# Where one modulation vector's matrix-vector product is computed: layer 1's mixer gate, in the recurrence or in layer 0's second channel product

## The chip, the core and the metric

The kernel runs on one core of a Trainium2 chip. The core has five engines that run side by side, each through its own queue of instructions in order: TensorE (PE; the loading of its stationary operand is listed apart as PEld), VectorE (DVE), ScalarE (ACT), GpSimd (POOL) and SyncE (SP), which here only issues DMA transfers. Data comes from DRAM into an on-chip memory of 128 partitions; matmul results go to banks of a second, small memory (PSUM) and are fetched from there by VectorE or ScalarE.

The metric is device time in microseconds (us), lower is better. Three timed runs of the kernel before gave 2395.1, 2395.52 and 2399.87 us, median 2395.52.

## The reference

A trunk of two layers on x (1 sequence × 1024 positions × 1024 channels, float32). Each layer has a token mixer (layer 0: softmax attention with forgetting; layer 1: gated linear attention, a recurrence over chunks) and a channel mixer of 2816 hidden channels. Both are fed a normalised input that is shifted and scaled, and their results are gated, by six vectors that are computed from a conditioning vector c:

```python
c_act = silu(c)
for i in range(2):
    mod = c_act @ ada_w[i] + ada_b[i]          # ada_w[i]: 1024 x 6144
    sh1, sc1, g1, sh2, sc2, g2 = split(mod, 6)
    h = rms_norm(x, norm1_g[i]) * (1 + sc1) + sh1
    y = forgetting_attention(h, ...) if i == 0 else gated_linear_attention(h, ...)
    x = x + g1 * y
    h = rms_norm(x, norm2_g[i]) * (1 + sc2) + sh2
    gate, up = split(h @ ffn_w_in[i], 2)
    x = x + g2 * ((silu(gate) * up) @ ffn_w_out[i])
return rms_norm(x, final_g)
```

So there are 12 modulation vectors of 1024 numbers, each a product of c_act with a 1024 × 1024 block of `ada_w` (4 MB). They depend on c alone and may be computed at any time before their use. The one at issue is (layer 1, j = 2): g1 of layer 1, which multiplies the recurrence's output projection.

## The kernel before

**Precision.** A float32 matmul is made of three products of a reduced type: each operand is split into a high part (a cast on ScalarE, line 174) and a low part (a subtraction on VectorE, line 175), and `mm3` (lines 286 to 288) adds high·high, high·low and low·high. So nearly every weight and activation passes through ScalarE and VectorE before TensorE can use it.

**Stages.** Layer 0's attention ends before 690 us of the profiled execution. Its channel mixer's first product runs to about 1012 us, its second product to about 1180, and the rest of that mixer, with the norm for the next layer, to about 1290. The recurrence of layer 1 follows, with its last head up to about 1690. Layer 1's channel mixer takes what is left.

**The channel mixer, `ffn`.** Both products use a scheme of seven block products in place of eight, with sums and differences of blocks as operands (names such as T1, T2, B11). The first product runs through groups of hidden channels, `for X in gs[2:]`. A finished hidden block is written to DRAM (`hid_d`). The second product runs over three chunks of hidden channels, the third of them followed by four hidden tiles that are multiplied plainly; a chunk makes 28 products (`p_`), each of 9 matmuls (3 × `mm3`). While one chunk is multiplied, the operands of the next are read back from `hid_d` by `part(c_)`: most directly into their tile (line 1607), those that still need a split through a ring of raw views, `late_raw` (split in line 1382 or 175). `late_raw` has four views: three in `tmpv`, and `opr_["u"][0]`, one slot of the operands of the first product that is free by then. The same ring serves `load_xr` (line 1631), which reads the mixer's input back for the final addition. The weights come through `feed`, some products ahead, as a raw view `xv` that is split into `o`. The results `p_b` are added up on VectorE (line 1521 in the first product, 1698 in the second) or copied out by ScalarE.

**A modulation vector, `ada_steps(l, j, acc, raw_of, nt, ahead)`.** On the paths at issue nt is 2, and a vector takes 32/nt = 16 steps. A step takes a raw view of 128 × 512, issues four loads of 64 KB into it on SyncE's queue (line 423), and then makes two multiply-adds on VectorE, 128 × 256 each (line 442 for a vector's first, line 444 for the others), which add `raw × c` to the sum `acc`. `ahead` is the number of steps whose loads are issued before the first multiply-add: with `len(raws_)` raw views it is one less. After 16 steps two small matmuls with a 128 × 4 operand of ones (`mp`, line 449) sum over the partitions, and one addition on VectorE (line 452) puts the vector into `modc`.

**Pace.** The steps are a generator that the main work drives. `Pace` counts units of TensorE's work: each product of the channel mixer calls `ada1(0.64 * n)`, 1.92 units for a product of 9 matmuls, and the recurrence calls `ada1(5.1)` once per projection. A step costs `ADA_A` units before its multiply-adds and `ADA_B` after them; `flush` runs all that is left at once. The multiply-adds are tied behind the VectorE instruction that was written last (`issue_after(last_of("D"))`).

**Where each vector of layer 1 is computed before.** j = 0 and 1 in layer 0's first channel product (`mid(0, 1)`, three raw views, pace 6.0 + 3.0); j = 2, 3 and 4 in the recurrence (`ada1_queue((2, 3, 4), ...)`, two raw views, pace 2.6 + 1.0); j = 5 in layer 1's first channel product (pace 12 + 6).

**What sets the order.** The program is written as one stream. A scheduler then puts the instructions of each engine into an order, with a simulated timeline, keeping the dependences between tiles and the ties that the code states. SyncE's loads go out in that order too. A change in one place can thus move instructions elsewhere.

**The recurrence.** Per head: projections (`gv_body`, `head_front`, `r_proj`), the gate with its exponentials and logarithms on ScalarE (lines 1859 and 1860) and a scan on VectorE (line 1864), a state `Sf` that is updated on VectorE (line 1942) and split for TensorE (`S_t`), and an output `on_t` (line 1990) that is transposed by TensorE (line 1952).

## Time and profile before

| | |
|---|---|
| median of three runs | 2395.52 us (2395.1 to 2399.87) |
| the profiled execution, its own time | 2397.77 us |
| its span in the profile | 2396.1 us |
| granted TensorE clock, mean | 0.997 |
| busy: PE, VectorE, ScalarE, GpSimd | 2368.3, 1776.6, 1127.8, 1008.5 us |
| DMA | 363.42 MB, mean 152 GB/s |

The profile is one execution. It gives for each engine the time in which it was busy, and for a group of instructions (one source line, one operation, one pair of tiles) the count, busy sum and mean. Tile names say what is moved: `ad_s` is the raw view and the sum of a modulation vector, `p_b` a product in PSUM, `xv_s` a raw weight, `o_s` a split weight. A row of a window's table gives, for a stretch of the span, the busy time of each engine. Rows of the timeline give start, duration, engine, line and operation; a bracket at the end tells the idle time before an instruction and what ended it. A row of waits reads: engine and waiting instruction, what released it, and then the idle time in us, the number of such waits and the longest. A row of DMA issues gives count, size and the median time from issue to landing.

### The profile page before, as it was taken

The numbers are of one execution on the slowest core, as the hardware profiler recorded it, in microseconds if no ns is written. First come the engines' busy times: TensorE is split into PE (matmuls) and PEld (weight loads), VectorE is DVE, ScalarE is ACT, GpSimd is POOL, SyncE is SP. The second block draws the span as 40 slices with busy tenths as digits, with TensorE's granted clock in tenths as the row PEclk, the third lists the DMA queues.
The fourth block names the chain that finished last, engine by engine and source line by source line (L and its number), as shares of the span: only waits on it lengthen the run. The fifth ranks groups of instructions, "written<-read, shape, count | busy, mean of one in ns | idle before, by whom it ended". The sixth has DMA issues, their size and how long they took to land.

```text
span 2396.1 us, 35784 instructions
## 1 busy us (share of the span) xinstructions
PE 2368.3 (99%) x12344; PEld 2016.8 (84%) x12344; DVE 1776.6 (74%) x3016; ACT 1127.8 (47%) x2164; POOL 1008.5 (42%) x911
## 2 busy tenths in 40 slices
PE   8999999999999999999999999999999999999998
PEld 7888888888888888888888888898888888888888
DVE  6577878886698788876798666655687877775787
ACT  6666555674443333345325645353343333345326
POOL 1333333333445666643264321222345666643262
PEclk9999999999999999999999999999999999999999
DMA  7422424342435544557655242334424544457664
GB/s 254 145 89 90 131 84 128 106 138 83 150 109 173 179 166 165 171 196 261 229 187 162 67 119 80 107 112 135 136 96 161 183 145 159 154 182 256 228 202 146
DMA packets 335773, 363.42 MB, mean 152 GB/s; under 512 B 24348, under 2 KB 277432, under 8 KB 335592
## 3 DMA queue, kind: packets, MB, share of 16 engines
q1 hardware_dynamic: 335592, 361.15, 45.9%
q8 instruction: 97, 1.59, 0.3%
q14 instruction: 84, 0.69, 0.1%
HBM read 268.19 MB, written 92.86 MB: 151 GB/s over the span
## 4 chain that ended last, share of the span: by engine, by line
PE 90%; DVE 5%; DMA 2%; ACT 1%; issue 1%; POOL 0%; SPq 0%; DVEq 0%; POOLq 0%; ACTq 0%
PE p_b L288 16%; PE p_b L286 16%; PE p_b L287 16%; PE t_b L1164 2%; PE o_b L1178 2%; PE qk_b L286 2%; PE qk_b L287 2%; PE qk_b L288 2%; PE vps_b L286 1%; PE vps_b L288 1%; PE vps_b L287 1%; PE s_b L1132 1%; PE s_b L1133 1%; PE gr_b L286 1%; PE gr_b L287 1%
## 5 line engine op out<-in xcount | busy, mean ns | idle before, releaser
L175 DVE TENSOR_TENSOR o_s<-xv_s,o_s 128x512 fp32r<-128x512 f32 (+1 forms) x376 | 324.1, 867 | 66.1 <-ACT o_s L174 65.6
L174 ACT CAST o_s<-xv_s 128x512 fp32r<-128x512 f32 (+1 forms) x376 | 216.2, 587 | 303.6 <-PE p_b L288 248.0
L287 PE MATMUL p_b<-B,o_s 128*128 128x512 f32 x608 | 237.8, 391 | 0.0
L288 PE MATMUL p_b<-B,o_s 128*128 128x512 f32 x608 | 237.5, 391 | 0.0
L286 PE MATMUL p_b<-B,o_s 128*128 128x512 f32 x608 | 236.3, 392 | 0.0
L1144 POOL TENSOR_SCALAR lp_s<-lp_s,st 128x128 f32<-128x128 f32 (+7 forms) x128 | 99.0, 778 | 291.1 <-DVE st L1143 280.7
L843 POOL TENSOR_TENSOR ex_s<-xv_s,xv_s 128x512 f32<-128x512 f32 (+1 forms) x64 | 85.5, 1335 | 292.8 <-DMA xv_s<-in_ffn_w_in_dram 120.7
L286 PE MATMUL p_b<-T,o_s 128*128 128x512 f32 x480 | 186.7, 389 | 0.0
L287 PE MATMUL p_b<-T,o_s 128*128 128x512 f32 x480 | 186.7, 389 | 0.0
L288 PE MATMUL p_b<-T,o_s 128*128 128x512 f32 x480 | 181.2, 389 | 0.0
L287 PEld LDWEIGHTS p_b<-B,o_s 128*128 128x128 f32 x608 | 115.0, 189 | 23.9
L286 PEld LDWEIGHTS p_b<-B,o_s 128*128 128x128 f32 x608 | 115.0, 189 | 23.8
L288 PEld LDWEIGHTS p_b<-B,o_s 128*128 128x128 f32 x608 | 114.7, 189 | 24.0
L1142 ACT ACTIVATE lp_s<-lp_s,st 128x128 f32<-128x128 f32 (+7 forms) x128 | 99.3, 777 | 65.2 <-DVE st L1138 62.1
L174 ACT CAST pt_s<-t_b 128x512 fp32r<-128x512 f32 (+1 forms) x160 | 79.7, 547 | 75.4 <-PE t_b L1164 73.9
L845 POOL TENSOR_TENSOR xv_s<-ex_s,xv_s 128x512 f32<-128x512 f32 (+1 forms) x64 | 88.1, 1377 | 60.7 <-DVE o_s L175 58.2
L1521 DVE TENSOR_TENSOR ex_s<-ex_s,p_b 128x512 f32<-128x512 f32 x140 | 93.7, 681 | 23.4 <-PE p_b L288 23.2
L227 POOL TENSOR_TENSOR w_l_s<-w__s,w_h_s 128x256 fp32r<-128x256 f32 x90 | 69.7, 803 | 94.7 <-ACT w_h_s L223 56.7
L175 DVE TENSOR_TENSOR pt_s<-t_b,pt_s 128x512 fp32r<-128x512 f32 (+1 forms) x160 | 96.2, 631 | 15.9 <-ACT pt_s L174 15.3
L287 PEld LDWEIGHTS p_b<-T,o_s 128*128 128x128 f32 x480 | 90.1, 188 | 18.7
L286 PEld LDWEIGHTS p_b<-T,o_s 128*128 128x128 f32 x480 | 90.1, 188 | 18.7
L288 PEld LDWEIGHTS p_b<-T,o_s 128*128 128x128 f32 x480 | 90.1, 188 | 18.6
(1954 smaller groups left out, 7392.9 us busy)
## 6 DMA issues: line engine op xcount, KB each, us to landing
xv_s<-in_ffn_w_in_dram SPq DMA_DIRECT2D x176, 256.0 KB, 3.3
hid_B<-x SPq DMA_DIRECT2D x70, 512.0 KB, 2.6
ad_s<-in_ada_w_dram SPq DMA_DIRECT2D x384, 64.0 KB, 2.4
hid_T<-x SPq DMA_DIRECT2D x36, 512.0 KB, 2.8
xv_s<-in_ffn_w_out_dram SPq DMA_DIRECT2D x96, 192.0 KB, 5.3
ada_s<-in_ada_w_dram SPq DMA_DIRECT2D x128, 128.0 KB, 2.8
xv_s<-in_ffn_w_out_dram SPq DMA_DIRECT2D x40, 256.0 KB, 2.9
T2o<-hid_T SPq DMA_DIRECT2D x18, 512.0 KB, 8.4
```

The source lines that it names most:

```text
L174: nc.scalar.copy(hi, src)
L175: nc.vector.tensor_sub(lo, src, hi.bitcast(F32))
L227: (nc.gpsimd if i < 3 else nc.vector).tensor_sub(lo[:, cs], rw[:, cs], hi[:, cs].bitcast(F32))
L286: nc.tensor.matmul(ps, ah, bh, start=start, stop=False)
L287: nc.tensor.matmul(ps, ah, bl, start=False, stop=False)
L288: nc.tensor.matmul(ps, al, bh, start=False, stop=stop)
L843: nc.gpsimd.tensor_add(s1, a21, a22)
L845: nc.gpsimd.tensor_sub(a11, s1, a11)
L1142: nc.scalar.activation(lp, lp, AF.Exp, bias=mcur, scale=-1.0, accum_out=st[:, qi, 2:3])
L1144: nc.gpsimd.tensor_scalar(lp, lp, st[:, qi, 3:4], 1.0, op0=ALU.mult, op1=ALU.mult)
L1164: nc.tensor.transpose(tp[:, i, :], lps[qi][:, psl(2 * b + jj)], ident)
L1521: nc.vector.tensor_add(d, d if src is None else dest(G, src), ps)
```

## The change

Vector (layer 1, j = 2) leaves the queue of the recurrence and becomes a queue of layer 0's `ffn`, started at the last but one group of its first product and driven by the products of the second. There it has one raw view, the slot half `opr_["u"][0]`, and `opr_["u"][1]` holds the sum; so `ahead` is 0, and a step's loads can only go out when the multiply-adds of the step before have read the view. Its pace is 5.0 + 2.5 units. A flush before the last chunk makes sure that it is done. `late_raw` loses that view and has three; `load_xr`, which comes later, has the four as before. The recurrence keeps j = 3 and 4, with the pace 4.0 + 1.4 in place of 2.6 + 1.0. The tests on `ahead` in `ada_steps` become tests on `nt`, so that a vector with `ahead` = 0 still yields before its multiply-adds.

```diff
-            if ahead:
+            if nt == 2:
                 yield ADA_A
             raw = got.popleft()
             with ExitStack() as es:
-                if ahead:
+                if nt == 2:
                     es.enter_context(tc.issue_after(last_of("D")))
...
-            yield ADA_B if ahead else 1.0
+            yield ADA_B if nt == 2 else 1.0
...
-    def ada1_queue(js, acc, raws_):
+    def ada1_queue(ljs, acc, raws_):
         r = Cycle(raws_)
-        for j in js:
-            ada1.q.append(ada_steps(1, j, acc, r, 2, len(raws_) - 1))
+        for l, j in ljs:
+            ada1.q.append(ada_steps(l, j, acc, r, 2, len(raws_) - 1))
...
-    def ffn(l, oh, xs, slots, nm, mid, norm_end, each=None):
+    def ffn(l, oh, xs, slots, nm, mid, norm_end, each=None, later=()):
...
-        late_raw = Cycle(list(tmpv) + [opr_["u"][0]])
+        late_raw = Cycle(list(tmpv))
+        xr_raw = Cycle(list(tmpv) + [opr_["u"][0]])
...
-                    xr[(a, hf)] = late_raw()
+                    xr[(a, hf)] = xr_raw()
...
             if X is gs[-2]:
                 ada1.flush()
+                if later:
+                    ada1_queue(later, opr_["u"][1][:, 0:256], opr_["u"][0:1])
+                    ada_rate(5.0, 2.5)
                 nxt[0] = part(0)
                 advance(4)
...
         for c_ in range(OC):
             last = c_ == OC - 1
+            if last:
+                ada1.flush()
...
+    def ada_rate(a, b):
+        nonlocal ADA_A, ADA_B
+        ADA_A, ADA_B = a, b
...
-    ffn(0, oh, xs, slots, "fo", lambda: mid(0, 1), norm_mixer)
+    ffn(0, oh, xs, slots, "fo", lambda: mid((1, 0), (1, 1)), norm_mixer, later=((1, 2),))
...
-    ada1_queue((2, 3, 4), ada_v[0][:, 0:256], ada_v[1:3])
-    ADA_A, ADA_B = 2.6, 1.0
+    ada1_queue([(1, j) for j in (3, 4)], ada_v[0][:, 0:256], ada_v[1:3])
+    ADA_A, ADA_B = 4.0, 1.4
```

More of the change, by code (lines that the diff above doesn't have):

```diff
@@ L1760, in norm_mixer, with mid @@
         return gates
-    def mid(*js):
-        v = Views(slots["hid"], 2, [HALF], f"ad{js[0]}").v
-        ada1_queue(js, v[0][:, 0:256], v[1:4])
+    def ada_rate(a, b):
+        nonlocal ADA_A, ADA_B
+        ADA_A, ADA_B = a, b
+    def mid(*ljs):
+        v = Views(slots["hid"], 2, [HALF], f"ad{ljs[0][0]}").v
+        ada1_queue(ljs, v[0][:, 0:256], v[1:4])
     ADA_A, ADA_B = 6.0, 3.0
-    ffn(0, oh, xs, slots, "fo", lambda: mid(0, 1), norm_mixer)
+    ffn(0, oh, xs, slots, "fo", lambda: mid((1, 0), (1, 1)), norm_mixer, later=((1, 2),))
     h1 = hs1
@@ L2102, in trunk @@
     ADA_A, ADA_B = 12.0, 6.0
-    ffn(1, oh, xs, slots, "go", lambda: mid(5), final_norm, final_scale)
+    ffn(1, oh, xs, slots, "go", lambda: mid((1, 5)), final_norm, final_scale)
     dump("xb1", xs)
```

## The prediction, made before the changed kernel was run

> **What bounds the kernel now.** The page comes first: span, busy time, and the chain of work that ended last.
>
> ```profile
> span 2396.1 us, 35784 instructions
> ...
> PE 2368.3 (99%) x12344; PEld 2016.8 (84%) x12344; DVE 1776.6 (74%) x3016; ACT 1127.8 (47%) x2164; POOL 1008.5 (42%) x911
> ...
> PE 90%; DVE 5%; DMA 2%; ACT 1%; issue 1%; POOL 0%; SPq 0%; DVEq 0%; POOLq 0%; ACTq 0%
> ```
>
> TensorE bounds the program: 28 us of the span have no matmul in them. A change that adds and removes no large matmul can only win back such idle time, or make more of it. So the second view is the busy time by stage (us, then each engine with its count, granted clock, DMA share, GB/s). The stages are layer 0's first channel product, its second product, the end of that mixer, and the recurrence up to its last head.
>
> ```profile
> core 0: us, PE busy (x) PEld busy (x) DVE busy (x) ACT busy (x) POOL busy (x), PEclk, DMA share, GB/s
> 690.00:1012.00 322.00, 322.00 (x1426) 266.72 (x1425) 266.61 (x353) 121.73 (x214) 198.41 (x132) 1.00 0.52 173
> 1012.00:1180.00 168.00, 168.00 (x742) 139.08 (x742) 112.30 (x159) 69.74 (x132) 68.15 (x54) 1.00 0.61 218
> 1180.00:1290.00 110.00, 109.43 (x489) 90.24 (x489) 98.21 (x138) 38.44 (x71) 51.46 (x41) 1.00 0.61 199
> 1290.00:1600.00 310.00, 306.15 (x1888) 274.46 (x1887) 198.48 (x363) 159.37 (x340) 81.30 (x94) 0.99 0.35 101
> ```
>
> The stage that gives the work away, 1290 to 1600, has 310.00 − 306.15 = 3.85 us of PE idle time: the whole prize. The stage that takes it, 1012 to 1180, has none: there the change can only be free or cost. Its VectorE is idle for 168 − 112.3 = 55.7 us.
>
> **The change, part by part.** First, what the gate g1 of layer 1 costs where it is. The rows of the modulation tile within the recurrence:
>
> ```profile
> L423 SPq DMA_DIRECT2D ad_s<-in_ada_w_dram x192: 560/592/1827, 1302.2 to 1586.0; - x192
> L444 DVE SCALAR_TENSOR_TENSOR ad_s<-ad_s,c,ad_s x48: 467/485/1049, 1344.9 to 1589.3; 128x256 f32<-128x256 f32 x48
> L444 DVE SCALAR_TENSOR_TENSOR ad_s<-ad_s,c x45: 461/484/1054, 1343.1 to 1587.5; 128x256 f32<-128x256 f32 x45
> ...
>   DMA ad_s<-in_ada_w_dram: 25.9, 14
> ...
> DMA to landing us min/median/max: 2.2/2.4/6.5
> ```
>
> Three vectors make 192 loads and 96 multiply-adds there; one third leaves: 64 loads (64 × 0.592 = 37.9 us of SyncE's issuing) and 32 multiply-adds (32 × 0.485 = 15.5 us of VectorE). VectorE also sat idle 25.9 us, 14 times, for these loads; with the slower pace of the two that stay (4.0 + 1.4 for 2.6 + 1.0, one load ahead as before), a load has 9.4 units instead of 6.2 before its use, so most of these waits go too. What is that worth to PE? The PE waits of the stage, and what ended them:
>
> ```profile
> PE go_b L286 <- ACT S_t L174: 1.4, 1, 1.4
> PE ogt_b L1952 <- DVE on_t L1990: 1.1, 2, 0.8
> PE go_b L286 <- ACT junk L1986: 1.0, 1, 1.0
> PE gr_b L286 <- DVE gvt_s L175: 0.4, 1, 0.4
> ```
>
> None is ended by a modulation instruction. The queue of ScalarE ahead of the 1.4 us wait (PE at 1398.07):
>
> ```profile
> 1393.00 1.28 ACT L1859 ACT_TABLE_LOAD   x1
> 1394.29 1.06 ACT L1859 ACTIVATE t_s<-t_s 128x1024 f32<-128x1024 f32 x1
> 1395.37 1.28 ACT L1860 ACT_TABLE_LOAD   x1
> 1396.66 1.06 ACT L1860 ACTIVATE t_s<-t_s 128x1024 f32<-128x1024 f32 x1
> 1397.63 0.39 ACT L174 CAST S_t<-Sf 128x256 fp32r<-128x256 f32 x1
> ...
> 1403.10 0.41 ACT L174 CAST S_t<-Sf 128x256 fp32r<-128x256 f32 x1 [2.94 <-DVE Sf L1942]
> ```
>
> Two table loads and two gate functions (4.7 us) stand in front of the cast of the state. The 1.0 us wait has the same source: the cast at 1403.10 came late because VectorE ran the gate's scans:
>
> ```profile
> 1400.29 2.33 DVE L1864 TENSOR_TENSOR_SCAN b_s<-ad_s,t_s 128x512 f32<-128x512 f32 x2
> ```
>
> A multiply-add of 0.485 us stands between such steps only here and there. So lighter VectorE work in the recurrence gives at most 3.85 us back and, from these rows, little of it; the other end is a new wait as long as the longest shown, +1.4, because the program's order in this stage is made anew. I take −0.5, near the rows that name the gate as cause. The cover of the 32 multiply-adds that went was PE's own work; nothing else was late for them.
>
> Second, the cost where the gate goes. The pace is 5.0 + 2.5 units a step, 16 steps, from the last but one group of the first product until about 1180. There is one buffer (the other half of a slot holds the sum), so a step's four loads wait for both multiply-adds of the step before, and its multiply-adds wait for the loads: nothing is fetched ahead. The first step's loads stand far ahead in SyncE's queue and cost nothing. One round is 3 × 0.592 + 2.4 = 4.2 us of loading and about 1 us of VectorE, against some 8 us of PE time a step (7.5 units; 1.92 units are one product of 9 matmuls, 2.04 us). VectorE gets 15.5 us of work more and, in the built order, some ten of the fifteen later steps have their multiply-adds so close behind their loads that VectorE will stand about 2 us, 20 us in sum. 15.5 + 20 = 35.5 of 55.7 idle us: it fits on the average. It must also fit where the lead is short. VectorE's low half of a weight, and PE's first use of it:
>
> ```profile
> 1067.37 0.69 DVE L1521 TENSOR_TENSOR sg_s<-sg_s,p_b 128x512 f32<-128x512 f32 x1 [2.04 <-PE p_b L288]
> 1068.03 0.69 DVE L175 TENSOR_TENSOR o_s<-xv_s,o_s 128x512 fp32r<-128x512 f32 x1
> ...
> 1071.48 0.39 PE L286 MATMUL p_b<-T,o_s 128*128 128x512 f32 x1
> ```
>
> This lead, 1071.48 − 1068.72 = 2.76 us, is the shortest that I found in the stage. In the changed order the fourth step's first multiply-add stands between these two VectorE rows. The first step's pair stands behind the first row here, an evacuation between the two; the other rows are of SyncE's queue:
>
> ```profile
> 1048.99 0.69 DVE L175 TENSOR_TENSOR o_s<-xv_s,o_s 128x512 fp32r<-128x512 f32 x1
> ...
> 1060.64 0.91 SPq L1607 DMA_DIRECT2D B11o<-hid_B  x2
> ...
> T2o<-hid_T SPq DMA_DIRECT2D x5, 512.0 KB, 8.4
> xv_s<-in_ffn_w_out_dram SPq DMA_DIRECT2D x13, 192.0 KB, 7.0
> ```
>
> Walked on: step 1's pair ends at 1049.7 + 0.5 + 0.7 + 0.5 = 1051.4. Step 2's loads then go, with a spill between them, and are in at 1056.4 (4.2 and the spill's turn); its pair, with an evacuation between, ends at 1058.1. Step 3's loads are in at 1062.5 (4.2 us on), its pair ends at 1063.5. Step 4's loads go out from 1063.6, behind three loads of 512 KB into B11o, and from there on the DMA engines are full: the last two rows are the times from issue to landing between 1050 and 1100.
>
> With only those three in front of it I put step 4 in at 1069.2 (5.6 us after its first issue, between 2.4 and 8.4, nearer the middle since the larger loads that made the 8.4 now come after it). Then 0.49 and 0.69: the weight is ready at 1070.4, 1.1 us before its use. So no PE wait by this walk, and 3.5 us at the upper end: last issue 1065.4 + 8.4 = 1073.8, ready at 1075.0.
>
> In the same place SyncE is held: the loads behind step 4's go out some 4 us later. Of those the last pieces of T2o had least time in hand:
>
> ```profile
> 1069.75 1.12 SPq L1607 DMA_DIRECT2D T2o<-hid_T  x2
> ...
> 1081.68 0.39 PE L286 MATMUL p_b<-T2o,o_s 128*128 128x512 f32 x1
> ```
>
> 1081.68 − 1069.75 − 8.4 = 3.5 us. Issued 4 us later they would be late by half a us, but the built order also puts PE's use of them about 4 us later, behind a product that is ready, so I take 0.
>
> Third, PE itself: the two small matmuls that sum the vector now stand in PE's queue between
>
> ```profile
> 1181.64 0.39 PE L286 MATMUL p_b<-T1o,o033s_s 128*128 128x512 f32 x1
> 1181.87 0.39 PE L287 MATMUL p_b<-T1o,o033s_s 128*128 128x512 f32 x1
> ```
>
> and wait there for the last multiply-add, which VectorE has behind these:
>
> ```profile
> 1176.33 0.55 DVE L175 TENSOR_TENSOR o_s<-xv_s,o_s 128x384 fp32r<-128x384 f32 x1
> 1177.76 0.69 DVE L1698 TENSOR_TENSOR x<-x,p_b 128x512 f32<-128x512 f32 x1 [0.88 <-PE p_b L288]
> ```
>
> Steps 14 to 16 follow each other in rounds of 5.5 to 6 us, so I walk the last multiply-add to 1180.6, 1.3 us ahead; all matmuls behind it would wait if it were late. Bounds 0 to 2.
>
> Fourth, the raw ring of the second product shrinks from four views to three, and the last chunk's T4 pieces are fetched later. VectorE's first split of one, and the first use:
>
> ```profile
> 1185.64 1.50 DVE L1382 TENSOR_TENSOR T4o<-ex_s,T4o 128x512 fp32r<-128x512 f32 x1
> ...
> 1204.08 0.39 PE L286 MATMUL p_b<-T4o,o_s 128*128 128x512 f32 x1
> ```
>
> 18 us of cover; I take 0. The flush before the last chunk finds an empty queue, and the gate's user, the output projection after the recurrence, is far away: 0.
>
> Sum: −0.5 in the recurrence (−3.85 to +1.4), +1.5 in the second product for the two thin places together (0 to +3.5 at the first, 0 to +2 at the second, and as much again if the second busy stretch of the DMA has a like place): +1.0. The profiled execution took 2397.77 us for its span of 2396.1, 2.25 above the median of the runs; on the median, 2395.5 + 1.0 = 2396.5.
>
> [...]
>
> **Rivals.** A, slower: in the busy stretches a step's loads land as late as the rows of 8.4 us say; VectorE, which takes its work in order, stands, and PE waits 3.5 us at 1071 and as much in the busy stretch that follows at 1133 to 1156: +7.0 − 0.5, 2402.0. It decides from the point where step 4 lands after 1070.3; each us beyond is a us of PE. For it: 8.4 and 7.0 above. Against it: the DMA engines have only 1.5 MB of operands in front of step 4. B, faster: the new order of the recurrence, with 15.5 us less on VectorE and most of the 25.9 us of waits gone, loses all PE waits: −3.85, 2391.7. Against it: no wait there is ended by the modulation. C: the summing matmuls hold PE's queue for 2 us: 2397.0 with no other loss. That the change does nothing it says is not open: the built order moves the 32 multiply-adds.
>
> [...] This trace has a half-rate stretch with no idle time at all ahead of it, 5.00 × (1 − 0.66) = 1.7 us:
>
> ```profile
> 1303.00:1308.00 5.00, 5.00 (x31) 5.00 (x32) 1.98 (x5) 1.56 (x4) 3.74 (x4) 0.66 0.67 199
> ```
>
> **How the numbers follow.** Forecast 0.53, A 0.22, B 0.13, C 0.12. What a measurement of this kernel can tell from no change is about 0.2%, 4.8 us. A lies beyond it; B alone does not reach it (3.85) and does with a little luck in the clock, so half of B counts as faster: 0.07 faster, 0.22 slower, 0.71 the same. The range runs from B's end, 2391.5, to A's with the half-rate stretch, 2404.0.
>
> **What would show it.** Right: PE busy still 168 of 168 us at 1012 to 1180; no PE wait ended by a split of a weight near 1071; VectorE busy there near 128 us, with some 20 us of idle time ended by loads of the modulation weights; in the recurrence 128 loads, 64 multiply-adds, waits for loads well below 25.9 us, and the PE waits on the gate's casts still there. Wrong: a PE wait of over 2 us at 1071 or at the summing matmuls, or a recurrence with PE busy all through.

## The result, and the profile after

The changed kernel takes 2404.84 us (median of 5 runs, 2403.76 to 2408.42); the kernel before, with two more runs, takes 2398.6 us (2395.1 to 2399.87). The ratio is 1.0037, with a 95% interval of 1.0023 to 1.0051: slower by about 9 us in the interval's middle, by 6.2 us as a difference of the medians. The profiled executions differ by 5.9 us of span, and the ledger below is made for these 5.9 us. The forecast was 2396.5 us and no difference that can be measured. It was wrong, and the time lies just outside the range.

From the page of the changed kernel, the span, the busy times, and the chain of work that ended last by engine:

```profile
span 2402.0 us, 35766 instructions
...
PE 2370.2 (99%) x12344; PEld 2017.1 (84%) x12344; DVE 1776.5 (74%) x3016; ACT 1126.0 (47%) x2164; POOL 1011.9 (42%) x911
...
PE 81%; DVE 8%; DMA 5%; ACT 3%; issue 2%; SPq 1%; POOL 0%; DVEq 0%; POOLq 0%; ACTq 0%
```

VectorE's busy time is what it was (1776.5 against 1776.6 us) with as many instructions: the work has only moved. The chain has lost 9 points of TensorE, most of them to VectorE and transfers, so there are now places where TensorE waits. The busy time by stage says where (columns as in the prediction; the windows are the same, while the program runs later in the last two):

```profile
1012.00:1180.00 168.00, 163.65 (x708) 133.82 (x707) 117.30 (x176) 65.99 (x127) 64.77 (x51) 0.98 0.72 237
1180.00:1290.00 110.00, 107.82 (x474) 87.88 (x473) 98.18 (x142) 33.55 (x64) 49.24 (x37) 1.00 0.58 187
1290.00:1600.00 310.00, 307.56 (x1903) 276.27 (x1902) 189.38 (x339) 163.64 (x345) 89.20 (x101) 0.99 0.32 96
```

TensorE idles 4.35 us between 1012 and 1180, where it had idled 0, and 2.18 us between 1180 and 1290, where it had idled 0.57. In the recurrence its idle time fell by 1.4 us, from 3.85 to 2.44.

For an exact ledger I cut both programs at the same instructions. The second product runs from the first matmul with B11o to the first with f0e01800p_b. These are two rows of before's timeline of TensorE, then the same two of after's:

```profile
1076.92 0.39 PE L286 MATMUL p_b<-B11o,o_s 128*128 128x512 f32 x1
...
1252.03 0.47 PE L286 MATMUL f0e01800p_b<-hh,oo_s 128*128 128x512 f32 x1 [0.32 <-issue]
```

```profile
1077.26 0.39 PE L286 MATMUL p_b<-B11o,o_s 128*128 128x512 f32 x1
...
1263.12 0.47 PE L286 MATMUL f0e01800p_b<-hh,oo_s 128*128 128x512 f32 x1 [0.29 <-issue]
```

So the second product takes 1252.03 − 1076.92 = 175.1 us before and 185.9 us after. (The prediction and the section on the kernel before put this product at 1012 to 1180. The rows show the first product's last groups running until about 1077, so the window of 1012 to 1180 covers the end of the first product and 60% of the second.) With the other cuts, in us (the third cut is the first matmul of layer 1's channel mixer, at 1730.9 before and 1739.5 after):

| stretch | before | after | difference |
|---|---|---|---|
| up to the second product | 1076.9 | 1077.3 | +0.3 |
| second product | 175.1 | 185.9 | +10.8 |
| end of the mixer, recurrence | 478.9 | 476.3 | −2.6 |
| all of layer 1 behind it | 665.2 | 662.6 | −2.6 |

Sum: +5.9. Of the −2.6 in the last row, 1.6 is chance in the clock (the last section); nothing was changed there. The change costs 10.8 us where the gate went and returns 2.6 us where it was.

What TensorE waited for in after between 1012 and 1290 (us in total, times, longest); before has two waits of 0.3 there:

```profile
PE p_b L286 <- ACT o032s_s L174: 2.1, 1, 2.1
PE p_b L288 <- DVE o_s L175: 1.4, 2, 0.9
PE p_b L288 <- DVE o032s_s L175: 1.3, 1, 1.3
PE p_b L286 <- DVE ex_s L1521: 0.9, 2, 0.7
PE mp_b L449 <- DVE ex_s L444: 0.5, 1, 0.5
```

The largest place is one weight, o032s, at 1169 to 1174. After's timeline of TensorE there, and of the engines that make the weight:

```profile
1171.40 0.67 PE L286 MATMUL p_b<-T1o,o032s_s 128*128 128x512 f32 x1 [2.12 <-ACT o032s_s L174]
...
1173.82 0.80 PE L288 MATMUL p_b<-T1o,o032s_s 128*128 128x512 f32 x1 [1.33 <-DVE o032s_s L175]
1174.41 0.63 PE L286 MATMUL p_b<-T1o,o032s_s 128*128 128x512 f32 x1
```

```profile
1169.81 0.99 POOL L843 TENSOR_TENSOR ex_s<-xv_s,xv_s 128x384 f32<-128x384 f32 x1 [15.53 <-DMA xv_s<-in_ffn_w_out_dram]
1170.83 0.51 ACT L174 CAST o032s_s<-ex_s 128x384 fp32r<-128x384 f32 x1 [13.24 <-POOL ex_s L843]
1170.95 1.20 DVE L444 SCALAR_TENSOR_TENSOR ex_s<-ex_s,c 128x256 f32<-128x256 f32 x1 [6.95 <-DMA ex_s<-in_ada_w_dram]
1173.22 0.54 DVE L175 TENSOR_TENSOR o032s_s<-ex_s,o032s_s 128x384 fp32r<-128x384 f32 x1
```

Two things meet. GpSimd and ScalarE had long been free (15.53 and 13.24 us idle): the weight's raw data came late. And VectorE, which makes the weight's low half, had stood 6.95 us at a multiply-add for its load. The first cost TensorE 2.1 us, the second 1.3 us, and the matmuls then ran at half rate until 1178 (0.63 us each, where 0.39 us is usual; starts 0.43 us apart where 0.23 us is usual; the granted clock from 1171 to 1178 is 0.54): some 2.2 us more. From the starts of the matmuls, the 10.8 us are 4.0 (these two waits) + 2.2 (half rate) + 1.3 (1080 to 1083, behind late evacuations) + 0.7 (summing matmuls) + 1.3 (1255 to 1258), and 1.3 that I could not put in a place.

Why was the raw data late? SyncE's own waits between 1040 and 1180, first of before, then of after. L825 loads the raw weights of this product, L1608 (before: L1607) the operands, L423 the modulation:

```profile
SPq L825 <- DVE o_s L175: 52.9, 22, 9.3
```

```profile
SPq L825 <- DVE o_s L175: 6.9, 5, 2.4
...
SPq L423 <- DVE ex_s L444: 4.2, 2, 3.4
SPq L423 <- DVE x L1704: 3.9, 1, 3.9
...
SPq L423 <- DVE o032s_s L175: 3.7, 1, 3.7
SPq L423 <- DVE o_s L175: 3.2, 2, 2.0
```

The row with L825 is SyncE being early: it waits for a buffer to come free. Before, it had 52.9 us of such lead; after, 6.9. Two costs took it. One is issuing, as after's rows on the modulation tile show (the three numbers are shortest, median and longest in ns); the other is the rows with L423, where SyncE is held because VectorE has not yet come past its reading of the single buffer:

```profile
L423 SPq DMA_DIRECT2D ex_s<-in_ada_w_dram x60: 560/567/997, 1052.4 to 1187.4; - x60
...
  DMA ex_s<-in_ada_w_dram: 33.8, 13
```

60 × 0.567 = 34 us of issuing, and 15.0 us in the four rows quoted with L423: 49 us together, and 46.0 us of the lead are gone. The second row here is VectorE standing 33.8 us for these loads, 13 times. What the lost lead does is seen at the reload of the operands for the second chunk, in SyncE's timeline of before and then of after (the last two rows of before's are the raw weight of o032s and GpSimd's start on it):

```profile
1125.39 0.34 SPq L1607 DMA_DIRECT2D B21o<-hid_B  x1
...
1144.19 1.62 SPq L1607 DMA_DIRECT2D T2o<-hid_T  x2
...
1149.33 0.38 SPq L825 DMA_DIRECT2D xv_s<-in_ffn_w_out_dram  x1
...
1157.44 1.31 POOL L843 TENSOR_TENSOR ex_s<-xv_s,xv_s 128x384 f32<-128x384 f32 x1 [8.58 <-DMA xv_s<-in_ffn_w_out_dram]
```

```profile
1132.34 0.58 SPq L1608 DMA_DIRECT2D B21o<-hid_B  x1
...
1145.17 4.40 SPq L423 DMA_DIRECT2D ex_s<-in_ada_w_dram  x4
...
1158.50 0.62 SPq L1608 DMA_DIRECT2D T2o<-hid_T  x1
...
1160.96 0.38 SPq L825 DMA_DIRECT2D xv_s<-in_ffn_w_out_dram  x1
1162.21 3.74 SPq L423 DMA_DIRECT2D ex_s<-in_ada_w_dram  x4
```

The reload starts 7 us later, and its last piece goes out 13 us later (the second of before's x2 at 1145.5, after's at 1158.5). The raw weight of o032s goes out behind it, at 1160.96 where before it was 1149.33: 11.6 us later. From its issue to GpSimd's start it takes 8.1 us before and 8.9 after, so it is late because it was issued late, not because its own transfer took longer. Before, its cast (1158.78) ended 8 us ahead of its first use (1167.36). The modulation loads that VectorE stands for go out right behind it, at 1162.21. Meanwhile the DMA engines are full, and move less than in before's full stretch. The rows by 10 us (last two columns: DMA share, GB/s), before and then after:

```profile
1140.00:1150.00 10.00, 10.00 (x46) 8.29 (x45) 6.12 (x11) 2.47 (x5) 4.36 (x4) 1.00 1.05 387
...
1160.00:1170.00 10.00, 10.00 (x46) 8.29 (x45) 7.23 (x13) 2.87 (x6) 3.28 (x4) 1.00 0.26 79
```

```profile
1150.00:1160.00 10.00, 10.00 (x46) 8.29 (x45) 6.60 (x13) 3.30 (x7) 4.04 (x4) 1.00 1.03 321
1160.00:1170.00 10.00, 9.28 (x41) 7.33 (x40) 4.00 (x8) 0.00 (x0) 0.19 (x1) 1.00 1.02 332
```

Before, the burst is over by 1160; after, it is still in full course when o032s is due.

### The profile page after: what moved, and what is told of

Read it like the earlier page. It is cut to its first block, busy times and chain, and to the rows that moved or that the text cites. A ratio compares the mean times of both kernels' runs of the same rounds, so it can differ in the third digit from the quotient of the medians.

```text
span 2402.0 us, 35766 instructions
## 1 busy us (share of the span) xinstructions
PE 2370.2 (99%) x12344; PEld 2017.1 (84%) x12344; DVE 1776.5 (74%) x3016; ACT 1126.0 (47%) x2164; POOL 1011.9 (42%) x911
## 4 chain that ended last, share of the span: by engine, by line
PE 81%; DVE 8%; DMA 5%; ACT 3%; issue 2%; SPq 1%; POOL 0%; DVEq 0%; POOLq 0%; ACTq 0%
PE p_b L287 15%; PE p_b L286 15%; PE p_b L288 15%; PE o_b L1178 2%; PE t_b L1164 2%; PE qk_b L286 1%; PE qk_b L288 1%; PE qk_b L287 1%; PE vps_b L286 1%; PE vps_b L288 1%; PE gr_b L286 1%; PE vps_b L287 1%; PE gr_b L287 1%; PE gr_b L288 1%; DMA adas_s<-in_ada_w_dram 1%
## 5 line engine op out<-in xcount | busy, mean ns | idle before, releaser
L1521 DVE TENSOR_TENSOR ex_s<-ex_s,p_b 128x512 f32<-128x512 f32 x140 | 93.5, 680 | 22.4 <-PE p_b L288 22.3
```

The source lines that it names most:

```text
L1521: nc.vector.tensor_add(d, d if src is None else dest(G, src), ps)
```

## The experiments

The theories to tell apart: the loss lies (a) in VectorE's added work, (b) in VectorE standing for its loads with nothing fetched ahead, (c) in the loads as 64 more entries of SyncE's queue, (d) in the loads' bytes. All runs, with the ratio to the kernel before in the same session; the profile's second product and the stretch behind it (the cuts of the ledger); the time from the start of the second product to SyncE's last issue of T2o pieces in the reload ("reload"); and SyncE's lead (the row that was 52.9). Times in us. The last four columns are read from one profiled execution of each kernel, whose own time stands ahead of them. Where it lies far from the median (two buffers, one step ahead: 7.9 us below; none ahead: 5.3 above; in two bursts: 4.8 below; the eighths in place: 3.1 below), these columns do not show a middle execution.

| kernel | median | ratio, 95% | profiled run | second product | mixer end, recurrence | reload | lead |
|---|---|---|---|---|---|---|---|
| before | 2398.6 |  | 2397.77 | 175.1 | 478.9 | 68.6 | 52.9 |
| after | 2404.84 | 1.0037 (1.0023–1.0051) | 2403.76 | 185.9 | 476.3 | 81.2 | 6.9 |
| gate left out | 2392.81 | 0.998 (0.9971–0.9989) | 2393.25 | 174.1 | 475.7 | 68.6 | 53.5 |
| gate in both places | 2409.74 | 1.0044 (1.0031–1.0057) | 2409.74 | 187.1 | 479.6 | 81.6 | 7.0 |
| loads alone, waiting for nothing | 2398.28 | 1.0004 (0.9995–1.0013) | 2398.28 | 174.3 | 477.3 | 68.4 | 42.0 |
| multiply-adds alone | 2392.55 | 0.9977 (0.9968–0.9986) | 2392.36 | 174.6 | 476.6 | 68.6 | 50.4 |
| two buffers, one step ahead | 2404.2 | 1.0026 (1.0015–1.0037) | 2396.34 | 180.3 | 476.9 | 83.4 | 19.9 |
| two buffers, none ahead | 2401.64 | 1.002 (1.0009–1.003) | 2406.98 | 181.9 | 479.2 | 85.1 | 13.0 |
| gate in the first product | 2408.6 | 1.0045 (1.0033–1.0058) | 2406.69 | 179.5 | 476.9 | 74.7 | 51.7 |
| other pace | 2403.71 | 1.0028 (1.0016–1.0039) | 2403.04 | 183.9 | 477.3 | 81.8 | 6.0 |
| loads in place, no multiply-adds | 2402.91 | 1.0022 (1.0012–1.0032) | 2404.71 | 181.7 | 480.1 | 89.7 | 11.4 |
| loads of an eighth | 2404.67 | 1.0033 (1.0021–1.0046) | 2404.67 | 183.9 | 477.3 | 78.8 | 8.0 |
| eighths in place, no multiply-adds | 2399.43 | 1.0006 (0.9995–1.0016) | 2396.36 | 179.0 | 476.7 | 84.2 | 8.0 |
| in two bursts | 2406.29 | 1.0041 (1.0027–1.0054) | 2401.5 | 185.7 | 475.8 | 85.8 | 15.5 |
| one load a step | 2400.03 | 1.001 (1.0001–1.0019) | 2399.76 | 175.6 | 480.7 | 75.4 | 23.1 |
| one load, two buffers | 2400.3 | 1.001 (1.0001–1.0019) | 2399.93 | 176.0 | 479.8 | 69.1 | 31.4 |
| one load, all of layer 1 | 2402.58 | 1.0025 (1.0016–1.0034) | 2403.02 | 176.8 | 479.3 | 75.5 | 22.5 |
| one load, two buffers, held back | 2400.04 | 1.0009 (1.0–1.0018) | 2400.72 | 175.4 | 480.8 | 68.8 | 30.1 |
| before, held back | 2397.47 | 0.9995 (0.9987–1.0004) | 2397.97 | 174.4 | 479.4 | 67.7 | 53.9 |
| before, one load, all of layer 1 | 2409.44 | 1.004 (1.0027–1.0053) | 2410.32 | 176.0 | 485.2 | 69.2 | 51.0 |

**The gate left out, and in both places.** Two kernels that complete the square of "gate in the recurrence or not" and "gate in the second product or not".

```diff
-    ffn(..., norm_mixer, later=((1, 2),))
+    nc.vector.memset(modc[:, 1, 2], 1.0)
+    ffn(..., norm_mixer)
```

> The changed kernel without the moved vector: layer 1's mixer gate is set to ones and computed nowhere; the ring of three views and the lighter recurrence stay. The changed kernel took 2404.8 us, the kernel before 2398.6; in the profiled runs the changed kernel lies 10.6 us behind at the end of layer 0's channel mixer and wins 3.0 us back in the recurrence. Theory 1 (SyncE's queue is held by the single view's loads, so the operands and weights behind them come late): no PE wait of over 0.5 us in the second product, total 3 us below before, about 2395.5. Theory 2 (VectorE stands for the loads and is late with splits): the same. Theory 3 (4 MB more through a full DMA): the same. Theory 4 (the ring of three views makes the T3 and T4 pieces late): PE waits near 1081 and 1170 us stay, 2400 or more.

```diff
-    ada1_queue([(1, j) for j in (3, 4)], ada_v[0][:, 0:256], ada_v[1:3])
-    ADA_A, ADA_B = 4.0, 1.4
+    ada1_queue([(1, j) for j in (2, 3, 4)], ada_v[0][:, 0:256], ada_v[1:3])
+    ADA_A, ADA_B = 2.6, 1.0
```

> The changed kernel, but the recurrence computes the gate a second time, with the pace of before (three vectors, 2.6 + 1.0). If the recurrence gained its 3.0 us from the 32 multiply-adds that left, the gain is gone: about 2398.6 + 10 = 2408. If the gain is only a luckier order of the recurrence that any edit ahead of it could give, it may stay: about 2405.

The two edits add up. Taking the gate out of the recurrence, with the slower pace of the two vectors that stay, gives 478.9 − 475.7 = 3.2 us without the second product's part and 479.6 − 476.3 = 3.3 with it; putting it into the second product costs 185.9 − 174.1 = 11.8 and 187.1 − 175.1 = 12.0. The whole loss sits in the second product, and the ring of three raw buffers, which the first kernel has too, costs nothing (174.1 us, against 175.1 with four).

**Loads alone, and multiply-adds alone.**

```diff
-                for t in range(nt):
+                for t in range(nt if ahead or nt == 4 else 0):
```

> The changed kernel without the 32 multiply-adds of the second product: the 64 loads go out at the same places, but wait for no VectorE instruction; the gate is computed from a constant. Theory 1 (the hold in SyncE's queue) and theory 2 (VectorE standing): no PE wait of over 1 us in the second product, 2395.5 to 2397. Theory 3 (the bytes, in the stretches where the DMA is full): most of the 4 us near 1170 stays, 2401 or more.

```diff
-            for q in range(4):
+            for q in range(4 if ahead or nt == 4 else 0):
```

> The changed kernel without the 64 loads of the second product: its 32 multiply-adds read a view filled once with a constant. Theories 1 and 3: no PE wait of over 0.7 us in the second product, 2395.5 to 2396.5. A theory 2 in which VectorE's 15.5 us of extra work alone make splits late: the waits near 1081 and at the summing matmuls stay, 2397.5 to 2400.

The multiply-adds alone cost 0.5 us against the gate left out (174.6 to 174.1); TensorE waits nowhere in that product, so this is the time of the summing matmuls themselves. Their row of 1012 to 1180, TensorE without a gap and VectorE with 128.64 us:

```profile
1012.00:1180.00 168.00, 168.00 (x744) 139.10 (x744) 128.64 (x191) 69.59 (x131) 68.73 (x54) 1.00 0.62 220
```

So (a) falls. The loads alone do not isolate what they were meant to: with nothing to wait for, all 64 went out between 594 and 656 us, in layer 0's attention and none in the second product, and what comes before that product became 5.6 us longer. That run decides nothing on (c).

**Buffers and pace.** Two buffers with a step fetched ahead, the same without fetching ahead, and the same total pace in another split:

```diff
-    ada1_queue(later, opr_["u"][1][:, 0:256], opr_["u"][0:1])
+    ada1_queue(later, sm.tile([P, 256], F32, tag="t1k", name="gacc"), opr_["u"])
```

> The changed kernel with two raw views for the second product's vector (the sum moves to a small tile of its own), and so one step loaded ahead. A step's loads are written behind the multiply-adds that read the same view 2.5 units before, as in the changed kernel; but VectorE comes to them a whole step later. Without the vector the kernel took 2392.8 us, with it 2404.8. Theory 1 (the hold in SyncE's queue): the hold stays, and with it most of the 12 us: 2400 or more. Theory 2 (VectorE standing for the loads): the PE waits near 1081 and 1170 us go, about 2393 to 2395.

> The same two raw views, but with no step loaded ahead: a step's loads wait for multiply-adds that lie a whole step and 2.5 units back, while VectorE comes to them after 5.0 units as in the changed kernel. Theory 1: SyncE is hardly held, the PE waits go, about 2393 to 2395. Theory 2: VectorE stands as before, 2400 or more.

```diff
-                    ada_rate(5.0, 2.5)
+                    ada_rate(2.0, 5.5)
```

> The changed kernel with the pace 2.0 + 5.5 in place of 5.0 + 2.5: the multiply-adds follow closer behind their loads, and the next step's loads later behind the multiply-adds. Theory 1: SyncE is held less, the loss shrinks, 2396 to 2401. Theory 2: VectorE stands longer in each step, the loss grows, 2407 or more.

In the profiled executions two buffers win 5.6 of the 11.8 us back with the step ahead (180.3) and 4.0 without it (181.9); waits of 2.5 and 2.4 us for the same weight o032s are left. VectorE's standing for the loads falls from 33.8 us to 8.1 and 8.5. But the first of these executions is 7.9 us below the median of its kernel and the second 5.3 above, and by the medians the kernel without the step ahead is not the slower one (ratios 1.0026 and 1.002, with overlapping intervals): no run shows that the step ahead is worth anything. The other pace changes the places (3.7 us in six waits for weights, 2.0 at the summing matmuls) and wins 2.0. A second buffer also ends most of SyncE's holds, so this does not price (b) by itself. Even by the execution that favours two buffers most, (b) is at most about half.

**The gate in the first product,** before the second, with pace 4.0 + 2.0:

```diff
-    ffn(0, oh, xs, slots, "fo", lambda: mid((1, 0), (1, 1)), norm_mixer, later=((1, 2),))
+    ffn(0, oh, xs, slots, "fo", lambda: mid((1, 0), (1, 1), (1, 2)), norm_mixer)
```

> The vector is computed in layer 0's first channel product with the other two (three raw views, pace 4.0 + 2.0), nothing in the second; the recurrence keeps two vectors. VectorE is busy there for some 15.5 us more, 282 of 322 us, and SyncE has the loads two steps ahead. Theories 1 and 2: no loss in that product, about 2393. A theory that any more work of VectorE in a channel product costs time: 2396 or more, with PE waits between 690 and 1012 us.

SyncE keeps its lead (51.7), but all up to the second product takes 9 us more (1086.0). The row of 690 to 1012 shows why: VectorE at 281.07 of 322 us, with TensorE waiting 7.7 us in thirteen waits for its additions of the results (L1521).

```profile
690.00:1012.00 322.00, 313.12 (x1368) 254.33 (x1366) 281.07 (x367) 116.40 (x203) 188.80 (x124) 1.00 0.53 175
```

The second product itself loses nothing here: between its cuts TensorE idles nowhere, and its 179.5 us hold 24 matmuls more, 5.4 us at 0.227 us each, which the new order has put behind the first cut. So some 14 us were lost ahead of it. In that stage the waits name (a); the loads were not taken apart from it there. The same work, another stage, another limit.

**Loads in place.** Each load is tied behind the SyncE instruction that precedes it in the order, so that it goes out where the changed kernel has it; the multiply-adds are left out. Then the same with an eighth of each load's bytes; and the whole gate with an eighth of the bytes.

```diff
+              with (tc.issue_after(last_of("S")) if nt == 2 and not ahead else ExitStack()):
                 nc.sync.dma_start(raw[32 * q:32 * q + 32], ...)
...
-                for t in range(nt):
+                for t in range(nt if ahead or nt == 4 else 0):
```

> The changed kernel without the second product's 32 multiply-adds (the gate comes from a constant), and now with each of its loads tied behind the load written before it, so that the 64 loads stand in SyncE's queue where the changed kernel has them (without that tie they had gone out elsewhere). They wait for no VectorE instruction, and none waits for them. Theories 1 (SyncE held) and 2 (VectorE standing): no loss in the second product, 2393 to 2395. Theory 3 (the 64 loads keep the DMA engines full for longer, and the weights behind them land late): the PE wait of some 2.5 us near 1165 us stays, with DMA share near 1 up to 1165, 2397 to 2402.

```diff
+              w = 32 if nt == 2 and not ahead else 256
-                nc.sync.dma_start(raw[32 * q:32 * q + 32], src[:, 256 * q:256 * q + 256]...)
+                nc.sync.dma_start(raw[32 * q:32 * q + 32, :, 0:w], src[:, 256 * q:256 * q + w]...)
```

> The 64 loads in place, tied as in the run of that name, each cut to an eighth of its bytes, and no multiply-adds: entries in SyncE's queue and nothing else. The gate comes from a constant. Theory 5: a loss in the second product near that of the run with full loads and no multiply-adds (6.7 us there), at least 4. Theory 3 (bytes): none, 2393 to 2394.

> The changed kernel with each of the 64 loads cut to an eighth (32 columns of 256); the rest of the view holds a constant. The order, the waits of SyncE for VectorE and of VectorE for the loads stay. Theory 3: the bytes are gone, so the loss is gone, 2393 to 2396. Theory 1: SyncE is still held by the multiply-adds, 2399 or more. Theory 2: VectorE stands for less time, as the loads land sooner, but still stands: 2395 to 2400.

With the loads in place and no multiply-adds, 7.6 us of the 11.8 are there (181.7 to 174.1). About 1.0 of them are the summing matmuls and a wait for the copy that stands in for the sum, which leaves 6.6 for the loads. TensorE's longest wait is for the same weight:

```profile
PE p_b L286 <- ACT o032s_s L174: 2.6, 1, 2.6
PE p_b L286 <- ACT o_s L174: 1.7, 1, 1.7
```

With an eighth of the bytes 4.9 us remain (179.0), of which the summing matmuls and that wait (1.2 us) are 1.9, so the loads cost 3.0 with almost no bytes. With the multiply-adds in place too, an eighth of the bytes saves 2.0 (183.9); but 3.9 us of what is left is one wait of the summing matmuls for the last multiply-add, so at the weights it saves more than that. With 64 loads, then, neither the number nor the bytes carries the loss alone: each has about half in these executions. The medians of the two kernels without multiply-adds, each against its own session's kernel before, say the same within the noise (1.0022 and 1.0006, against 0.998 for the gate left out).

**In two bursts.** The steps run only in the last products of each chunk, where the transfers are fewest (DMA share in before 0.12 from 1110 to 1120 us and 0.14 from 1170 to 1180, against 1.05 from 1140 to 1150), at pace 1.4 + 1.0, with two buffers:

```diff
+                        ada1.on = (14, 12, 99)[c_] <= 7 * i + j < 25
...
+                    ada_rate(1.4, 1.0)
```

> A kernel meant to beat both: two raw views with one step ahead, and the 16 steps only in the last products of the first and of the second chunk, where the profile of before shows the DMA engines at 0.1 to 0.6 of their time and VectorE at 4 to 7 of 10 us, 2.4 units a step. If full DMA stretches are what the steps collide with: no loss in the second product, 2393 to 2394. If any place in the second product costs, 2398 or more.

No gain: 185.7. In a burst VectorE's weights come late (3.0 us in six waits, 2.8 in two for ScalarE's part), and the reload is as late as in the others (85.8).

**One load a step.** 256 KB over 128 partitions instead of four loads of 64 KB over 32 partitions each; the vector is then summed in quarters, with eight small matmuls in place of two. This tests (c) with the bytes and the multiply-adds kept; the number of partitions that a load covers changes with it.

```diff
+            raw = raw_of([P, HALF], F32, ...).rearrange("p (t c) -> p t c", t=2)
+            c0, r0 = j * D + 256 * (n // 4), 256 * (n % 4)
+            nc.sync.dma_start(raw, ada_w[l, r0:r0 + 256, c0:c0 + 256].rearrange("(t p) c -> p t c", p=P))
```

> The changed kernel with the same place, pace and single view, but each step's 256 KB come in one load of 128 partitions in place of four of 32: a step takes 256 columns of two blocks of 128 rows, and a quarter of the vector is done after four steps (eight small matmuls in place of two). 16 loads stand in SyncE's queue, not 64; bytes, the size of a piece in DRAM (1 KB), multiply-adds and the waits between loads and VectorE are as in the changed kernel. Theory 5 (the loss is the 64 entries: each costs SyncE its issue time, and a place among the few loads in flight, whatever its size): the loss of 12 us against the kernel without the vector shrinks to 0 to 4, 2393 to 2397. Theories 1, 2 and 3: as the changed kernel, 2402 to 2405.

The loss falls from 11.8 to 1.5 us (175.6), still with a single buffer, and TensorE idles nowhere between the cuts: the 1.5 us are the small summing matmuls. The row of 1012 to 1180 has no gap, VectorE's share is the expected one, and the bytes are all there (241 GB/s; after had 237):

```profile
1012.00:1180.00 168.00, 168.00 (x750) 139.20 (x749) 125.96 (x191) 68.51 (x131) 68.35 (x54) 1.00 0.69 241
```

```profile
L470 SPq DMA_DIRECT2D ex_s<-in_ada_w_dram x15: 367/383/578, 1051.6 to 1167.4; - x15
```

15 × 0.383 = 5.7 us of issuing stand where there were 34. The raw weight of o032s goes out at 1155.70, and its cast at 1163.61 is 4.9 us ahead of its use. SyncE is still held at the single buffer (12.7 us in ten waits for a multiply-add, near the 15.0 quoted of after), and VectorE still stands 14.8 us for the loads, in ten waits. So neither these holds nor (b) alone make the loss. All the bytes, VectorE's work and the single buffer are there, and TensorE loses nothing: this bears (c) out, as a matter of the number or of the form of the loads; which of the two, the runs do not tell. Against the gate left out the second product takes 1.5 us more, where after takes 11.8 more.

The kernel as a whole is still not faster than before (1.001), because the recurrence gives nothing back. At its start TensorE now waits for gvt_s, which VectorE makes (0.4 us of wait on gr_b before, 0.7 in after):

```profile
PE gr_b L286 <- DVE gvt_s L175: 4.4, 1, 4.4
```

**Can that be had as well?** Four more kernels: one load with two buffers; that form for all vectors of layer 1; two buffers with the first two steps of the recurrence's modulation held back behind SyncE's other loads; and that holding back in the kernel before. Then before with one load a step for all vectors of layer 1.

```diff
-                    ada1.q.append(ada_cols(1, 2, (u1[:, 0:256], u1[:, 256:512]), Cycle([u0]), 0))
+                    ada1.q.append(ada_cols(1, 2, (gacc0, gacc1), Cycle(opr_["u"]), 1))
```

> One load a step, two raw views and one step ahead: meant to beat both kernels. Theory 5: no loss in the second product, 2393. If VectorE standing or SyncE held is still worth something, this run is below the one with a single view by that.

> One load a step for all of layer 1's vectors, in the first channel products and in the recurrence too; the place of the moved vector as in the changed kernel with its single view. SyncE's queue has 288 entries fewer in all. Theory 5: as with one load for the moved vector alone, or 1 to 3 us lower from the recurrence, 2391 to 2397.

```diff
+              with (tc.issue_after(last_of("S")) if (l, j) == (1, 3) and n < 2 else ExitStack()):
```

> One load a step and two views in the second product, and besides the recurrence's first two steps of loads tied behind the loads written before them, so that they no longer stand ahead of the recurrence's first weights in SyncE's queue. With one load a step the second product had lost nothing in PE waits, but a wait of 4.1 us for the first gate projection of the recurrence (at about 1317 us, its operands late behind the cast of a late weight) had eaten the gain. If that wait comes from the entries ahead of the weight: gone, 2395 to 2396.5, below the kernel before. If from the transfers themselves: it stays, 2400.

> The kernel before with that tie alone. Its wait there was 0.55 us: at most that is gained, 2397.5 to 2398.1; a changed order in the recurrence may move it by a few us either way.

> The kernel before (three vectors in the recurrence) with one load a step for all of layer 1's vectors: 288 entries fewer in SyncE's queue, the multiply-adds as they were. If the recurrence's waits were due to the number of loads: down to 2394 to 2396. If to the order on ScalarE and VectorE, as the rows of before name it: no change, 2397 to 2400, or slower by what the four small sums per vector hold up.

None beats the kernel before. Holding back the modulation's first loads leaves the wait for gvt_s at 4.1 us, so these are not its cause; what is stays open. (TensorE also comes to it earlier in these kernels, which have no half-rate stretch just ahead of it: the granted clock of the some 15 us ahead is 1.00 where it was 0.89 in before and after.) In before, one load a step for all of layer 1 is slower by 0.4%, with 6.3 us more in the stretch of the recurrence: the form that helps where SyncE is short of lead does not help everywhere. The kernels faster than before are only those that leave the gate or its loads out.

**What the column "reload" tells.** Where the last T2o pieces go out at most 75.5 us after the product's start, the second product costs at most 2.7 us more than with the gate left out (the gate in the first product too, once its 24 additional matmuls are taken off). Where they go out after 78.8 us or more, it costs 4.9 to 13.0. Within the late group the order does not follow this time, nor the lead: in two bursts had 15.5 us of lead left and lost 11.6, the eighths in place 8.0 and lost 4.9. What the runs separate is the number of loads from their bytes and from VectorE's work. They do not separate a load's issue time on SyncE from its place among the transfers in flight, since both fall with the number, and the one load also differs in its partitions; 64 loads over 128 partitions each were not run. The time that the DMA engines are busy does not order the losses: from 1040 us to some 5 us behind the product, their share times the length is 142 us with the gate left out, 150 with the eighths in place, 157 with one load a step and 167 with the full loads in place. The one load adds 15 us and loses nothing, the eighths add 8 and lose 3.0.

## Why the prediction was wrong

The step that failed is the second part's "SyncE is held: the loads behind step 4's go out some 4 us later … I take 0", with the flat 1.5 us for all the thin places together. The measured term is 10.8 us. What the runs showed in its place: SyncE's lead goes from 52.9 to 6.9 us, the reload of the operands ends 13 us later, and the raw weight behind it goes out 11.6 us later, so that TensorE waits for o032s and then runs at half rate (6.2 us together). On the median of all five runs of before (2398.6) the same sum would have given 2399.6 and a range up to 2407.1. So it is owed to the low median of the first three that the time lies outside the range; the step is wrong either way, +1.0 us against +6.2.

- **Which engine was budgeted.** The prediction counted VectorE's idle time (35.5 of 55.7 us) and found room. The multiply-adds alone show that room was indeed there. It never made the same sum for SyncE, which issues in the same stretch: 34 us of issuing and 15.0 of holds at the single buffer, against 52.9 us of lead. It had the issue time (0.592 us a load), and used it for the recurrence's saving and for the length of one round only. That sum, 49 us, would still just have fitted, as VectorE's did. It would have shown that hardly any lead is left for the place where the operands are reloaded.
- **How far it looked.** It walked the first four steps and followed one operand, the T2o pieces of the first reload, which were indeed in time. The reload for the second chunk, 50 us later, has 16 modulation loads among it (issued from 1124 to 1149), and there the delay is 7 to 13 us.
- **First thin place.** Step 4's data were put in at 1069.2, with 1073.8 as the upper end. The fourth step's multiply-add started late, at the upper end:

```profile
1073.31 0.48 DVE L444 SCALAR_TENSOR_TENSOR ex_s<-ex_s,c 128x256 f32<-128x256 f32 x1 [4.38 <-DMA ex_s<-in_ada_w_dram]
```

TensorE did not wait for the weight at 1071, but for VectorE's late evacuations behind it (0.9 us, L1521, in the waits above).
- **VectorE standing.** Some 20 us predicted, 33.8 us measured; the longest, 6.95 us, stands ahead of o032s.
- **Summing matmuls.** The last multiply-add was walked to 1180.6 and started at about 1190; TensorE waited 0.5 us, within the bounds of 0 to 2.
- **The ring of three.** 0 was right.
- **The recurrence.** −0.5 predicted, −2.6 measured, −3.2 and −3.3 in the square. The waits that the prediction thought would stay, because no modulation instruction ended them, fell from 3.9 us to 2.4. In after's recurrence:

```profile
PE ogt_b L1962 <- DVE on_t L2000: 1.5, 3, 0.8
PE gr_b L286 <- DVE gvt_s L175: 0.7, 1, 0.7
PE go_b L286 <- ACT junk L1996: 0.2, 1, 0.2
```

The two waits on the gate's casts (1.4 and 1.0) are now 0 and 0.2, the two others 0.7 us longer together: −1.5 by waits. The small matmuls that went with the vector are some 0.5 more; the remaining 0.6 I could not put in a place. The name of a wait's last releaser does not say what made that releaser late. VectorE's waits for the modulation there fell from 25.9 us to 1.6, as forecast.
- **The rivals.** A (2402.0; chance 0.22) is what happened, nearly in size and with its second place: the busy stretch behind the reload, 4.0 us and a half-rate stretch of 2.2. The upper end of the range adds 1.7 us to A for such a stretch, the length of the one at 1303; that a wait of 3.5 us brings it, no run shows. What the runs showed in its place: the 2.2 us in after, behind waits of 2.12 and 1.33 us, and with one load a step half rate from 1322 to 1327 (0.63 us a matmul), behind the wait of 4.4 us for gvt_s. A's mechanism was half of it: VectorE standing is there, but without the multiply-adds 6.6 us of the loads' cost remain. B (0.13) was half right for the recurrence, and C came with 0.5 us. The chance of slower, 0.22, was too low for a change that puts 64 entries into SyncE's queue, whose lead (52.9 us) had not been counted.

## What to carry to other kernels

Before work is moved into a stage, add up its demand on every queue that it passes, the DMA-issuing one too, whose room is the time it waits for buffers to come free (here 52.9 us, against 34 us of issuing and 15.0 of holds at a single buffer). A sum that just fits was not enough: with 49 us against 52.9 the second product lost 10.8. Count loads and not only bytes: 16 loads of 256 KB over 128 partitions cost 1.5 us here where 64 loads of 64 KB over 32 partitions cost 11.8. Walk the next burst of transfers as well as the first, for that is where the lead that was spent was missed here (the second reload, 7 to 13 us late).

## What the runs showed of the hardware that was not expected

**Issue time did not follow the bytes.** A load of 64 KB over 32 partitions took SyncE 567 ns, one of 256 KB over 128 partitions 383 ns, and one of 8 KB over 32 partitions was no cheaper than the first (585 ns), as the row of the eighths in place shows:

```profile
L425 SPq DMA_DIRECT2D ex_s<-in_ada_w_dram x64: 560/585/1752, 1052.0 to 1172.4; - x64
```

**What comes ahead of a half-rate stretch.** The prediction said that before's stretch at 1303 has no idle time ahead of it. What stands ahead of it are 24 matmuls of one column (2.74 us). The same stands in layer 1, where before fell to half rate (0.77 us for the next matmul, the ones behind it 0.63) and after, behind the same 24 matmuls, did not (0.49, then 0.40). TensorE's timeline of before, then of after:

```profile
1301.15 2.74 PE L712 MATMUL sp_b<-ones,se_s 128*128 128x1 f32 x24
...
1738.67 2.95 PE L712 MATMUL sp_b<-ones,ss_s 128*128 128x1 f32 x24
1741.48 0.77 PE L286 MATMUL p_b<-B,o_s 128*128 128x512 f32 x1
```

```profile
1747.22 2.73 PE L712 MATMUL sp_b<-ones,ss_s 128*128 128x1 f32 x24
1749.82 0.49 PE L286 MATMUL p_b<-B,o_s 128*128 128x512 f32 x1
```

That is the 1.6 us of chance in the ledger: the granted clock is 0.51 from 1741.5 to 1744.5 in before, and 1.00 from 1749.8 to 1752.7 in after. Half rate is seen behind idle time too: after's matmul at 1171.40 took 0.67 us behind an idle time of 2.12 us. And 2.7 to 3.0 us of one-column matmuls are followed by half rate in some places (2.74 and 2.95 us, both in before) and not in others (2.73 us, in after). What decides between them no run here shows.
